# Order of units and start conditions at the opening of the second half, in a one-core attention and retention layer

## Chip, cores and metric

One core of one Trainium2 chip runs the whole program. The metric is the time of one execution in microseconds on the device. The kernel before has a median of 1897.52 us over three runs (1894.42, 1897.52 and 1897.54).

## What is computed

One layer of a streaming encoder, for 2048 prompt tokens and 64 tokens of a running stream. A combined projection of the normalised input feeds differential attention (branch A), retention (branch B), a gate path for each and two merge gates. Cut from the reference:

```
h = rmsnorm(x, norm_g) @ w_in
qa, ka, va, za, qb, kb, vb, zb, ga, gb = jnp.split(h, _split_points(), axis=-1)
...
oa = diff_attn_prompt(qa, ka, va, lam, slopes)      # block-causal, 4 heads, two softmaxes each
ob, r_p = retention_prompt(qb, kb, vb, log_g)       # chunkwise recurrence, 4 heads
...
oa = (rmsnorm(oa, subln_g) * (1.0 - lam_init)).reshape(B, T, W_A) * jax.nn.silu(za)
ob = rmsnorm(ob).reshape(B, T, W_B) * jax.nn.silu(zb)
m = ga * (oa @ w_oa) + gb * (ob @ w_ob)
return x + m @ w_out
```

## The kernel before, in words

The kernel splits every fp32 operand in a high part and a low part (`h` rounded to the matmul's type, `l` the remainder) and adds three products (high times high, high times low, low times high). So each piece of a weight matrix costs a load into a staging buffer `ws` (256 KB; there are three of them), a cast on ACT that makes `wh` (line 727), and a subtraction on POOL that makes `wl` (line 748).

**Two halves.** The prompt is projected in two halves of 1024 tokens. In the first half most columns go through a Strassen-like scheme (`strassen`, line 989). In the second half (`w_stream`, list `seqs[1]`, line 2994) there are three kinds of units:

- a *wide* unit (`natural`): 512 columns of `w_in`, eight pieces of 128x512, and eight tiles of 128 tokens. A tile takes 24 matmuls of 512 columns (line 1137), three with each piece, so all eight pieces are needed within the first tile. The three wide units are the attention's v, k and q.
- a *plain* unit (`transposed`): 256 columns, four pieces of 128x2x256, and 24 matmuls for each group of 512 or 288 tokens. The first four plain units are retention's q and k.
- the *quad* at the end: the last five column blocks in seven products (line 1564).

The pieces wait in a pool of 12 `w` and 4 `wx` buffers, two for a piece, so eight pieces in all (`next_piece`). A unit gives its pieces back during its last tile.

**Beside the projection** run, on the same engines, the attention of the first half's queries and later of the second's (`attn_head`: scores at lines 1877 and 1878, the score table added and the maximum found by DVE at 1886, exponentials on ACT at 1917, transposes at 1989, products with V at 1967 to 1969) and retention in blocks of 128 tokens (`ret_block`: three row loads, scores at 2334, key transposes at 2339, products at 2358, 2368 and 2371, output transposes at 2407).

**What sets the order.** The program is written out by coroutines (`loop`, line 216). Each yields a time or a condition. `loop` resumes the first one, by priority, whose time is not after `self.pe`, the planner's own clock for TensorE. Instructions are recorded in that order, and each engine executes its list in that order. All loads and stores go through one list as well, that of SP (`ld`, line 280, and `st`, line 285): a DMA there is issued after all those ahead of it, and waits first for what it needs. The planner's constants touched here are `CALM` (18000 of its nanoseconds) and `LAND` (2000).

**Start conditions around the change.** `h_loader` loads K and V of the heads (line 280, into `K` and `V`); after the first head it waits for `CALM`. `ret_stream` waits for twice `CALM` after the first q, k and v columns are there, and then runs the first eight retention blocks, at most two at a time; the other eight follow when the second half's retention columns are done. `ret_block` has its first matmul recorded at the time that the planner gives to the landing of its rows. A query tile of attention is 256 queries of one head; `attn_head` loops over the four tiles of a head and half.

Of the kernel before, what the change touches and what calls it, by code (L numbers as in the profile page):

```python
# [43 lines left out]
LAND = 2000.0  # L44
# [3 lines left out]
CALM = 18000.0  # L48
# [124 lines left out]
class Hybrid:  # L173
# [1654 lines left out]
    def h_loader(self, half):  # L1828
        for h in range(4):
            yield from self.head_in(half, h)  # L1830
            yield from self.load_head(half, h)
            if half == h == 0:
                yield self.pe + CALM

    def chunks(self, nk):
        n = nk // 128
# [8 lines left out]
    def attn_head(self, half, h):  # L1845
        yield lambda: len(self.heads) > 0
        hd = self.heads.pop(0)
        ks = hd["ks"]
        yield hd["tk"]
        for p in range(4 * half, 4 * half + 4):  # L1850
            yield lambda: len(self.qs) > 0
            q, tq = self.qs.pop(0)
            yield tq
            pair = {"n": 0, "rows": [None, None], "e": [None, None], "t": 0.0}
            for b in range(2):
                yield from self.qk_block(h, p, b, ks, q, pair)
            self.give("q", self.pe + LAT)
            self.spawn(self.at_pv(h, p, hd, pair, p % 4 == 3), 1, "z")
        self.give("K", self.pe + LAT, 2 * (half + 1))

# [452 lines left out]
    def ret_block(self, k, t0, r, first):  # L2313
# [9 lines left out]
        self.ld(qt, self.qbT[:, :, t0:t0 + r].rearrange("h p t -> p h t"), 1 << 18)  # L2323
        self.ld(kt, self.kbT[:, :, t0:t0 + r].rearrange("h p t -> p h t"), 1 << 18)
        t = self.ld(vb, self.vbN[t0:t0 + r, :], 1 << 18)
        yield max(t, self.t_rt)
        tx = 0
        if not first:
            nc.gpsimd.tensor_mul(qx, qt, self.rxi[:, :, :r])
# [3 lines left out]
        for h in range(4):  # L2333
            nc.tensor.matmul(s3[:, h, :], kt[:, h, :], qt[:, h, :], start=True, stop=True)
            t = self.P(512)
# [38 lines left out]
        if first:  # L2374
            nc.vector.tensor_copy(state, up)
            t = self.V(512, tu)
        else:
            for h in range(4):
# [3 lines left out]
                t = self.V(128, max(tu, to))  # L2382
# [15 lines left out]
        t = self.V(80)  # L2398
# [3 lines left out]
        t = self.V(632, t2) + SLACK  # L2402
# [3 lines left out]
        for h in range(4):  # L2406
            nc.tensor.transpose(tp[:, r * h:r * h + r], o[:, 128 * h:128 * h + 128], self.ident[:r, :r])
            t = self.P(256)
        res = qk[:, 0:4 * r]
        nc.scalar.copy(res, tp)  # L2410
        t = self.A(4 * r, t)
        self.give(bank, t)
        yield t
        for h in range(4):
            rh = res[:, r * h:r * h + r]
            d3 = self.obT[h].rearrange("p (g c) -> p g c", c=GW)
            if r == 128:
                g0, c0 = t0 // 256, t0 % 256
                t = self.st(d3[:, g0, c0:c0 + 128], rh, 1 << 16)
            else:  # L2420
                t = self.st(d3[:, :, 256:GW], rh.rearrange("p (g c) -> p g c", c=8), 1 << 17)
# [12 lines left out]

    def ret_stream(self):
        yield lambda: "kqv00" in self.done
        yield self.pe + 2 * CALM
        yield from self.ret_some(0, 8)
        yield lambda: "ret1" in self.done
        yield self.marks["ret1"] + 6000  # L2440
        yield from self.ret_sample()
        yield from self.ret_some(8, 8)
        yield self.t_state
        self.st(self.o["ret_prompt"][0, 0].rearrange("h d e -> d h e"),
                self.state.rearrange("p (h e) -> p h e", h=4), 1 << 18)
# [513 lines left out]
    def w_stream(self):  # L2959
# [3 lines left out]
        m0, m1 = (None, "kqv0"), (None, "kqv1")  # L2963
# [7 lines left out]
        wide = [(va, lambda half: self.natural(half, self.fin_va(0, 4), False, True), True),  # L2971
                (ka, lambda half: self.natural(half, self.fin_qk("k", 0, 4), False, True), True),
                (qa, lambda half: self.natural(half, self.fin_qk("q", 0, 4), False, True), True)]
        first = [wva, wk, wq, m0, m1]
        seq = []
        early = [(vb, lambda half: self.natural(half, self.fin_vb(), False, True, True), True)]
# [10 lines left out]
        for base, dst, n in ((za, self.zaT, 2), (zb, self.zbT, 2), (ga, self.gaT, 4), (gb, self.gbT, 4)):  # L2987
            for g in range(n):
# [2 lines left out]
        later = [(vb, lambda half: self.natural(half, self.fin_vb(), False, True), True)]  # L2991
        plain = [(c0, lambda half, a=a: self.transposed(*a), False) for c0, a in again[:PLAIN]]
        c0s, args = zip(*again[PLAIN:])
        seqs = [first + early + seq, [plain[0], wide[0], plain[1], wide[1], plain[2], wide[2], m0, m1, plain[3],
                                      *later, (None, "nat"), (None, "ret"), *plain[4:],
                                      (c0s, lambda half: self.quad(args), "quad")]]
        self.order = [[(c[0], c[2] if len(c) > 2 else False) for c in q if c[0] is not None] for q in seqs]
# [64 lines left out]
    def z_stream(self):  # L3062
        yield lambda: len(self.fresh) == 3
        self.n_spv = 0
        yield from self.sample_attn()
        yield lambda: self.live["z"] == 0
        yield from self.attn_zone()
        self.spawn(self.ret_stream(), 5, "z")
        for half in range(2):
            yield lambda: f"kqv0{half}" in self.done  # L3070
            self.heads, self.qs = [], []
            self.spawn(self.h_loader(half), 0, "z")
            self.spawn(self.q_loader(half), 0, "z")
            for h in range(4):
                yield from self.attn_head(half, h)
        yield lambda: self.live["z"] == 0
        self.z1.close()
        self.z3 = self.es.enter_context(self.tc.tile_pool(name="p3a", bufs=1, side="right"))
        self.z3x = ExitStack()
        self.z3w = self.z3x.enter_context(self.tc.tile_pool(name="p3w", bufs=1, side="right"))  # L3080
        self.ogs = {(g, br, kp): [] for g in range(8) for br in range(2) for kp in range(2)}
        self.oput = 0
        self.wo = [[], []]
        self.spawn(self.out_prep(), 1)
# [115 lines left out]
```

## Time and profile before

| what | us |
|---|---|
| median of three runs | 1897.52 |
| the profiled execution | 1894.89 |
| its span, first to last instruction | 1893.1 |
| TensorE (PE) busy in the span | 1869.9 |
| VectorE (DVE) busy | 1341.6 |
| ScalarE (ACT) busy | 973.9 |
| GpSimd (POOL) busy | 670.9 |

The profiled execution takes 1.8 us more than its span. A busy time is a sum over instructions; on PE the matmuls overlap, so the time from one start to the next says more than an instruction's own duration. The lists "who waited for whom" give the idle time of an engine before an instruction, and what ended it. SP has no work of its own in this table: it only issues DMAs.

### The profile page before, as it was taken

How to read it: one execution, taken by the hardware profiler on the slowest of the kernel's cores; microseconds unless marked ns; L12 is line 12 of the kernel's file. 1: busy time of each engine (PE TensorE's matmuls, PEld its weight loads, DVE VectorE, ACT ScalarE, POOL GpSimd, SP SyncE). 2: the span in 40 equal slices, each digit the busy share in tenths (PEclk: the TensorE clock that was granted, in tenths of full speed). 3: DMA queues.
4: the chain of work that ended last, by engine and by line, in shares of the span. 5: the costliest groups of instructions: out<-in, count | busy, mean ns of one | idle time of the engine just before them, and what ended most of it. 6: DMA issues, size and time to landing. Idle time of an engine off the chain costs nothing.

```text
span 1893.1 us, 33045 instructions
## 1 busy us (share of the span) xinstructions
PE 1869.9 (99%) x11090; PEld 1647.9 (87%) x11090; DVE 1341.6 (71%) x3111; ACT 973.9 (51%) x2266; POOL 670.9 (35%) x729
## 2 busy tenths in 40 slices
PE   9999999999999899999999999999999999999999
PEld 7788888888888789888888899889999999999887
DVE  6765757657584767886477686578886869977664
ACT  6434544555434566555455565556666536654221
POOL 2420366555552112121311444432122646512442
PEclk9999999999999999999999999999999999999999
DMA  7654555666857867464522854945534998976542
GB/s 254 215 176 123 160 161 180 180 196 195 248 178 200 233 194 213 126 201 123 168 69 83 230 138 133 227 130 139 143 103 138 276 256 280 269 236 206 171 156 78
DMA packets 402556, 340.09 MB, mean 180 GB/s; under 512 B 85329, under 2 KB 348625, under 8 KB 401362
## 3 DMA queue, kind: packets, MB, share of 16 engines
q1 hardware_dynamic: 402386, 337.97, 61.4%
q8 instruction: 88, 1.44, 0.3%
q14 instruction: 82, 0.67, 0.1%
HBM read 218.27 MB, written 118.75 MB: 178 GB/s over the span
## 4 chain that ended last, share of the span: by engine, by line
PE 86%; DMA 6%; DVE 4%; SPq 1%; ACT 1%; issue 1%; POOL 1%; DVEq 0%; ACTq 0%; POOLq 0%
PE mm L1137 27%; PE mm L989 8%; PE tp L989 4%; PE at L1989 3%; PE s L1877 2%; PE s L1878 2%; PE s L989 2%; PE pv L1969 2%; PE pv L1968 2%; PE pv L1967 2%; PE mm L1564 2%; PE s L2793 1%; PE s L2791 1%; PE s L2792 1%; SPq L280 1%
## 5 line engine op out<-in xcount | busy, mean ns | idle before, releaser
L748 POOL TENSOR_TENSOR wl<-ws,wh 128x512 fp32r<-128x512 f32 x108 | 146.4, 1368 | 210.4 <-ACT wh L727 196.7
L1137 PE MATMUL mm<-wh,xh 128*128 128x512 f32 x504 | 204.2, 405 | 3.0 <-ACT wh L727 3.0
L1137 PE MATMUL mm<-wl,xh 128*128 128x512 f32 x504 | 198.5, 394 | 0.8 <-POOL wl L748 0.8
L1137 PE MATMUL mm<-wh,xl 128*128 128x512 f32 x504 | 198.7, 394 | 0.0
L1137 PE MATMUL mm<-xh,wh 128*128 128x288 f32 (+2 forms) x544 | 179.3, 330 | 0.0
L1137 PE MATMUL mm<-xl,wh 128*128 128x288 f32 (+2 forms) x544 | 175.7, 323 | 0.0
L1137 PE MATMUL mm<-xh,wl 128*128 128x288 f32 (+2 forms) x544 | 175.5, 323 | 0.0
L1917 ACT ACTIVATE row<-row,a_mx 128x1024 f32<-128x1024 f32 (+7 forms) x144 | 150.0, 1044 | 11.3 <-DVE a_mx L1896 11.2
L2005 DVE TENSOR_TENSOR atl<-at,ath 128x512 fp32r<-128x512 f32 (+1 forms) x144 | 92.9, 659 | 74.0 <-ACT ath L2003 73.8
L2003 ACT CAST ath<-at 128x512 fp32r<-128x512 f32 (+1 forms) x144 | 79.2, 564 | 110.4 <-PE at L1989 104.0
L1745 POOL TENSOR_TENSOR r_y<-r_y,r_sq 128x256 f32<-128x256 f32 x32 | 29.8, 931 | 286.0 <-DVE r_sq L1742 210.2
L856 POOL TENSOR_TENSOR wl<-ws,wh 128x256 fp32r<-128x256 f32 x64 | 55.2, 862 | 196.2 <-ACT wh L847 196.0
L1886 DVE CUSTOM_DVE_ANT_0 row<-s,dfar 128x512 f32<-128x512 f32 (+2 forms) x148 | 91.5, 632 | 37.5 <-PE s L1878 36.6
L1137 PEld LDWEIGHTS mm<-wh,xl 128*128 128x128 f32 x504 | 95.0, 188 | 21.6
L1137 PEld LDWEIGHTS mm<-wh,xh 128*128 128x128 f32 x504 | 95.1, 189 | 20.7 <-ACT wh L727 3.3
L1137 PEld LDWEIGHTS mm<-wl,xh 128*128 128x128 f32 x504 | 95.4, 189 | 18.4 <-POOL wl L748 1.2
L1137 PEld LDWEIGHTS mm<-xh,wh 128*128 128x128 f32 x544 | 102.5, 188 | 7.4
L1137 PEld LDWEIGHTS mm<-xl,wh 128*128 128x128 f32 x544 | 102.5, 189 | 7.1
L1137 PEld LDWEIGHTS mm<-xh,wl 128*128 128x128 f32 x544 | 102.4, 188 | 6.7
L1939 DVE SCALAR_TENSOR_TENSOR row<-row,a_w 128x1024 f32<-128x1024 f32 (+5 forms) x88 | 98.8, 1128 | 0.0
L1877 PE MATMUL s<-K,q 128*128 128x512 f32 (+3 forms) x241 | 91.7, 381 | 0.2 <-DVE a_acc L1886 0.2
L727 ACT CAST wh<-ws 128x512 fp32r<-128x512 f32 x111 | 66.9, 617 | 41.0 <-DMA ws<-in_w_in_dram 11.2
(543 smaller groups left out, 6077.3 us busy)
## 6 DMA issues: line engine op xcount, KB each, us to landing
ws<-in_w_in_dram SPq DMA_DIRECT2D x155, 256.0 KB, 3.5
q<-qT SPq DMA_DIRECT2D x128, 128.0 KB, 3.1
K<-kT SPq DMA_DIRECT2D x48, 256.0 KB, 4.6
V<-vN SPq DMA_DIRECT2D x24, 512.0 KB, 5.5
row<-in_x_prompt_dram SPq DMA_DIRECT2D x16, 512.0 KB, 4.5
wz<-in_w_in_dram SPq DMA_DIRECT2D x32, 256.0 KB, 4.2
row<-in_cache_k_T_dram SPq DMA_DIRECT2D x32, 256.0 KB, 3.3
row<-in_cache_v_diff_dram SPq DMA_DIRECT2D x32, 256.0 KB, 3.6
```

What stands on the lines that cost most here:

```text
L727: self.nc.scalar.copy(h, st)
L748: eng.tensor_sub(l, st, h.bitcast(F32))
L856: nc.gpsimd.tensor_sub(l[:, cs], src, h[:, cs].bitcast(F32))
L989: nc.tensor.matmul(ps, w[:, c], xs[x][c], start=bool(tag) and c == 0 and i == 0, stop=c == 3 and i == 2, skip_group_check=True)
L1137: nc.tensor.matmul(ps, p, q, start=c == 0 and i == 0, stop=c == KC - 1 and i == 2)
L1877: nc.tensor.matmul(ps, q1s, kk, start=True, stop=False)
L1886: nc.vector.tensor_tensor_reduce(out=row[:, k0:k0 + n], in0=ps, in1=tab, scale=-SLOPES[h], scalar=3.0e38, op0=ALU.add, op1=ALU.min, accum_ ...
L1917: nc.scalar.activation(u, u, AF.Exp, bias=mx, scale=-1.0, accum_out=lp[:, k:k + 1])
L1939: nc.vector.scalar_tensor_tensor(out=u0, in0=u1, scalar=w[:, 0:1], in1=u0, op0=ALU.mult, op1=ALU.add)
L1989: nc.tensor.transpose(at[:, w:w + 128], src, self.ident)
L2003: nc.scalar.copy(ah[:, :w], at[:, :w])
L2005: nc.vector.tensor_sub(al[:, :w], at[:, :w], ah[:, :w].bitcast(F32))
```

## The change

Four edits. (1) The second half opens with two plain units and then two wide ones, where plain and wide units took turns; from the third plain unit on the list is as before. (2) K and V of the second head are loaded when three query tiles of attention have had their scores recorded, and not `CALM` after the first head's. (3) Retention starts when four query tiles are recorded plus one `CALM`, and not after two `CALM`. (4) In every retention block the rows count as landing `LAND` later, so its first matmul is recorded later in the list.

```diff
@@ h_loader
             if half == h == 0:
-                yield self.pe + CALM
+                yield lambda: self.ntile >= 3
@@ attn_head
             self.give("q", self.pe + LAT)
+            self.ntile += 1
@@ ret_block
-        yield max(t, self.t_rt)
+        yield max(t, self.t_rt) + LAND
@@ ret_stream
         yield lambda: "kqv00" in self.done
-        yield self.pe + 2 * CALM
+        yield lambda: self.ntile >= 4
+        yield self.pe + CALM
@@ w_stream
-        seqs = [first + early + seq, [plain[0], wide[0], plain[1], wide[1], plain[2], wide[2], m0, m1, plain[3],
+        seqs = [first + early + seq, [plain[0], plain[1], wide[0], wide[1], plain[2], wide[2], m0, m1, plain[3],
                                       *later, (None, "nat"), (None, "ret"), *plain[4:],
                                       (c0s, lambda half: self.quad(args), "quad")]]
@@ z_stream
+        self.ntile = 0
```

Each engine executes as many instructions of each kind as before; only the order and the choice of buffers differ. Line numbers in the changed kernel: retention's and attention's lines (1877, 1878, 2334) are higher by one, lines behind `ret_stream` by two, lines behind `z_stream` by three; lines up to 1830, among them 727, 748, 1137 and 1564, keep their numbers.

**SP at the opening of the second half.** `K`, `V` and `q` rows are the attention's loads, here those of the second head and the next query tiles, `ws` rows are weight pieces (128x512 of a wide unit, 128x2x256 of a plain one), `qbT<-ev` are stores of a plain unit. Before:

```order
L280 DMA K<-kT_59 64x1024
L280 DMA K<-kT_60 64x1024
L280 DMA K<-kT_59 64x1024
L280 DMA K<-kT_60 64x1024
L280 DMA V<-vN_61 128x8x128
L280 DMA V<-vN_62 128x8x128
L280 DMA q<-qT_57 64x2x256 x2
L280 DMA q<-qT_58 64x2x256 x2
L280 DMA ws<-in_w_in_dram 128x512
```

The `ws` row is the eighth and last piece of the first wide unit. At the same place now:

```order
L280 DMA ws<-in_w_in_dram 128x512
L285 DMA qbT<-ev 128x32
L285 DMA qbT<-ev 128x256
L280 DMA ws<-in_w_in_dram 128x512 x2
L280 DMA K<-kT_59 64x1024
L280 DMA K<-kT_60 64x1024
L280 DMA K<-kT_59 64x1024
L280 DMA K<-kT_60 64x1024
L280 DMA V<-vN_61 128x8x128
L280 DMA V<-vN_62 128x8x128
```

Three weight loads (pieces 4 to 6 of a wide unit that now begins one plain unit later) stand ahead of the second head's K and V.

**SP at the end of the first wide unit.** Before, the unit that follows is plain; the `128x2x256` row is the last of its four pieces, and the `128x512` rows are of the wide unit after that:

```order
L285 DMA obT<-row 128x128 x4
L280 DMA ws<-in_w_in_dram 128x2x256
L280 DMA ws<-in_w_in_dram 128x512 x2
L285 DMA vN_61<-thi 128x512
L285 DMA out_v_prompt_dram<-raw 128x512
L280 DMA row<-qbT 128x4x128
L280 DMA row<-vbN 128x512
L285 DMA vN_62<-tlo 128x512
L280 DMA ws<-in_w_in_dram 128x512 x3
```

Now the second wide unit follows at once; the five `128x512` rows are its pieces 4 to 8, and the `V` rows are the loads of a later head:

```order
L280 DMA ws<-in_w_in_dram 128x512
L285 DMA vN_62<-tlo 128x512
L280 DMA ws<-in_w_in_dram 128x512 x2
L280 DMA V<-vN_61 128x8x128
L280 DMA V<-vN_62 128x8x128
L280 DMA row<-qbT 128x4x128
L280 DMA ws<-in_w_in_dram 128x512
L285 DMA vN_61<-thi 128x512
L285 DMA out_v_prompt_dram<-raw 128x512
L280 DMA ws<-in_w_in_dram 128x512
```

A wide unit's last five pieces are now loaded while the unit ahead of it is in its last tile, and two V loads stand between the third and the fourth of them.

**SP at the last retention block.** `row<-qbT` and `row<-kbT` are its rows, `obT` and `oaT` stores of branch results, `zbT` and `gaT` stores of plain units, `xd` stores of input sums. Before:

```order
L280 DMA q<-qT_57 64x2x256 x2
L280 DMA q<-qT_58 64x2x256 x2
L285 DMA oaT<-r_o 128x256
L280 DMA row<-qbT 128x4x128
L285 DMA zbT<-ev 128x4x8
L285 DMA zbT<-ev 128x256
```

Now:

```order
L285 DMA gaT<-ev 128x2x256
L285 DMA xd<-xa 128x4x96
L280 DMA row<-qbT 128x4x128
L285 DMA xd<-xs 128x4x96
L280 DMA row<-kbT 128x4x128
L285 DMA obT<-row 128x128 x4
L285 DMA gaT<-ev 128x4x8
L285 DMA gaT<-ev 128x256
L280 DMA q<-qT_57 64x2x256 x2
```

The four query loads no longer stand ahead of the block's last row load but behind it.

## The prediction

> **What bounds the kernel now.** First the page's busy shares, then the list of what PE waited for. The columns of the list are: waiting instruction, what came last, total us, times, longest.
>
> ```profile
> span 1893.1 us, 33045 instructions
> PE 1869.9 (99%) x11090; PEld 1647.9 (87%) x11090; DVE 1341.6 (71%) x3111; ACT 973.9 (51%) x2266; POOL 670.9 (35%) x729
> ```
>
> ```profile
> PE mm L1137 <- ACT wh L727: 3.0, 1, 3.0
> PE mm L1564 <- DVE ev L1584: 2.3, 3, 1.2
> PE s L2334 <- DMA row<-qbT: 1.8, 1, 1.8
> PE s L2334 <- DMA row<-kbT: 1.8, 1, 1.8
> PE mm L1564 <- DVE u L1584: 1.6, 2, 1.0
> PE tp L1877 <- DMA q<-qT: 1.5, 1, 1.5
> ...
> PE s L1564 <- DVE ev L1584: 1.0, 1, 1.0
> ...
> PE mm L1137 <- POOL wl L748: 0.8, 1, 0.8
> PE tp L1878 <- DMA q<-qT: 0.8, 1, 0.8
> ```
>
> PE is idle for 1893.1 - 1869.9 = 23.2 us of the whole span, and the change takes no matmul away. So an order of instructions can win only what stands in this list, and the clock that an idle stretch costs. 3.0 + 0.8 us of it is one stall at the opening of the second half, 1.8 + 1.8 us are two retention blocks, 1.5 + 0.8 us are query loads, and 4.9 us belong to the quad.
>
> I then went to each place in time order. The stretches below have start and length in us, then the busy time (and number) of PE, PEld, DVE, ACT and POOL, the granted clock, the DMA share and GB/s.
>
> ```profile
> 600.00:627.00 27.00, 24.72 (x164) 22.67 (x163) 14.59 (x62) 14.15 (x39) 3.74 (x3) 1.00 1.02 259
> 627.00:634.00 7.00, 3.16 (x13) 2.20 (x12) 4.35 (x11) 2.81 (x8) 2.50 (x2) 0.87 1.11 280
> 634.00:650.00 16.00, 16.00 (x120) 15.14 (x118) 12.13 (x30) 10.97 (x29) 1.97 (x2) 0.95 0.74 225
> 650.00:700.00 50.00, 50.00 (x297) 43.84 (x297) 36.01 (x116) 28.37 (x73) 5.17 (x5) 1.00 0.70 199
> 1405.00:1460.00 55.00, 53.41 (x423) 52.17 (x422) 39.44 (x79) 37.62 (x82) 17.00 (x13) 1.00 0.43 135
> ```
>
> From 650 us on PE is covered; before that stands the costly place. Its PE rows and the SP rows ahead of them (start, length, instruction; a wait stands in brackets):
>
> ```profile
> 617.64 0.40 PE L1137 MATMUL mm<-wh,xh 128*128 128x512 f32 x1
> 617.88 0.40 PE L1137 MATMUL mm<-wl,xh 128*128 128x512 f32 x1
> 618.11 0.40 PE L1137 MATMUL mm<-wh,xl 128*128 128x512 f32 x1
> ...
> 630.81 0.50 PE L1137 MATMUL mm<-wh,xh 128*128 128x512 f32 x1 [2.99 <-ACT wh L727]
> 632.15 0.80 PE L1137 MATMUL mm<-wl,xh 128*128 128x512 f32 x1 [0.85 <-POOL wl L748]
> ```
>
> ```profile
> 616.49 2.39 SPq L280 DMA_DIRECT2D K<-kT  x4
> 618.92 1.21 SPq L280 DMA_DIRECT2D V<-vN  x2
> 620.23 4.98 SPq L280 DMA_DIRECT2D q<-qT  x4
> 625.31 0.54 SPq L280 DMA_DIRECT2D ws<-in_w_in_dram  x1
> ```
>
> ACT's cast is named, but it had waited itself: SP issued the eighth weight piece of the first wide unit only at 625.31, after 2.39 + 1.21 + 4.98 = 8.6 us of K, V and query loads, some of which waited for their buffers. The matmul that needs the piece began at 630.81, 5.5 us after that issue. So the bound here is **the order of SP's list**, not ACT or POOL. Starts of matmuls with 512 columns are 618.11 - 617.88 = 0.23 us apart at full clock.
>
> **The change part by part.** *Plain units first, second head later.* Three of the first wide unit's last loads now stand ahead of the second head's K and V, and its remaining two come with over 6 us to spare before the matmuls that need them, by counting the PE rows between at their spacing. So this stall goes: 2.99 + 0.85 = 3.84 us. With it goes the lower clock behind it: the rows give 0.87 over 7 us and 0.95 over 16 us, or 7 x 0.13 + 16 x 0.05 = 1.7 us. Together **-5.5**. What is late next is the query loads' wait of 1.5 + 0.8 us just before, whose rows ahead are the same in both orders; I leave it as it is.
>
> *Retention's rows count as landing later.* The two blocks wait here:
>
> ```profile
> 1211.72 1.13 PE L2334 MATMUL s<-row 128*128 128x128 f32 x8 [1.84 <-DMA row<-kbT]
> 1248.24 1.13 PE L2334 MATMUL s<-row 128*128 128x128 f32 x8 [1.84 <-DMA row<-qbT]
> ```
>
> In the order before, the two smallest distances between the earliest place where SP can issue a block's rows and their first use, counted in PE's work, are 7.9 and 9.9 us, and these two blocks wait. In the changed order the smallest are 9.0 and 10.3, all others 12.5 or more. By the old waits 7.9 + 1.84 = 9.7 and 9.9 + 1.84 = 11.7 were needed. But part of that need was SP's: at the second block four query loads stood ahead of the row load.
>
> ```profile
> 1239.32 3.24 SPq L280 DMA_DIRECT2D q<-qT  x4
> 1242.66 0.54 SPq L285 DMA_DIRECT2D oaT<-r_o  x1
> 1243.31 0.38 SPq L280 DMA_DIRECT2D row<-qbT  x1
> ```
>
> These 3.24 us are behind the row load now. So I take both waits as gone, **-3.7** (bounds: -3.7 and 0). The cover is projection and attention matmuls that PE has to do anyway; if it is too thin, 1.84 us stay each.
>
> *A new neighbour: wide after wide.* Before, each wide unit was followed by a plain one, which needs four pieces. Now the second wide unit follows the first at once, and its first tile needs eight pieces while the buffers hold eight and are given back only in the first unit's last tile. The trace of before has no such switch, so I build it from groups. The groups' columns are busy time, mean ns of one, and idle time before them; the DMA row ends with the median landing time.
>
> ```profile
> L748 POOL TENSOR_TENSOR wl<-ws,wh 128x512 fp32r<-128x512 f32 x108 | 146.4, 1368 | 210.4 <-ACT wh L727 196.7
> ...
> L1745 POOL TENSOR_TENSOR r_y<-r_y,r_sq 128x256 f32<-128x256 f32 x32 | 29.8, 931 | 286.0 <-DVE r_sq L1742 210.2
> ...
> L727 ACT CAST wh<-ws 128x512 fp32r<-128x512 f32 x111 | 66.9, 617 | 41.0 <-DMA ws<-in_w_in_dram 11.2
> ...
> ws<-in_w_in_dram SPq DMA_DIRECT2D x155, 256.0 KB, 3.5
> ...
> V<-vN SPq DMA_DIRECT2D x24, 512.0 KB, 5.5
> ```
>
> With time zero at the start of the last tile: the matmuls of its second piece have run by about 3.5, so the cast (0.62) and the subtraction (1.37) of the new second piece end at 5.5. That frees a staging buffer for piece 5: issue 0.5, landing 3.5, so 9.5. Its w buffers come free only at about 10.8; cast and subtraction end at 12.8, and only then piece 8 can be loaded: 12.8 + 4.0 = 16.8, cast at 17.4. POOL is then still at piece 7 and an `r_y` row of 0.93, and the eighth subtraction ends at 20.5 to 21.3. PE has, from the tile's start to the use of that piece, 104 matmul rows in the changed order: 50 of 512 columns at 0.23 (11.6), 2 of 384 at 0.18 (0.4), 20 of 256 at 0.12 (2.4), 20 of 128 at 0.11 (2.2) and 12 of retention that take two passes (2.6), about 19.2 in all. So PE waits 1.3 to 2.1; I take **+1.7**. Two more ends: nothing, if the staging turns faster; and more, if the two V loads in SP's list are slow ahead of the last pieces. The chain has one such load:
>
> ```profile
> 604.63 8.48 DMA V<-vN
> ```
>
> Then piece 8 lands at 12.8 + 8.5 = 21.3 and is ready with 0.62 + 1.37 + 0.93 at 24.2, a wait of 5.0. A wait of 2.99 brought the clock's 1.7 us above, so that end is +6.7.
>
> The clock, against the rows: a wait of 2.99 us was followed by 0.87 and 0.95; both waits of 1.84 us lie in stretches at 1.00:
>
> ```profile
> 1208.00:1214.00 6.00, 4.16 (x37) 3.96 (x36) 1.98 (x6) 1.83 (x4) 4.23 (x10) 1.00 0.71 181
> 1246.00:1250.00 4.00, 2.16 (x16) 1.75 (x15) 1.47 (x1) 0.62 (x1) 1.39 (x2) 1.00 0.97 252
> ```
>
> The Trainium skill, "TensorE: Matmul & The Clock Gate", section "What's actually happening", says that the array falls back to half its clock after an idle window of about 3.4 us, with a window that runs freely. Here an idle time of 2.99 us, shorter than that window, was enough, so the measurement decides and the threshold lies between 1.84 and 2.99 us in this trace. By the page's window the wide switch's 1.7 us would cost no clock, and a 5.0 us wait an estimated 1.7 more; the sum is the same either way.
>
> *The quad.* Attention is delayed by the later second head and so lies longer beside the quad, whose matmuls waited for DVE: 55.00 - 53.41 = 1.6 us in 1405 to 1460. By the order, the quad's matmuls ahead of the last product with V go from 234 to 276 of 840, and the common stretch from about 50 to 65 us. At 1.6 us in 55 that is **+0.5**. Below it is bounded by -1.6 (attention's extra work fills what the quad waits for), above by +3, if the rate doubles.
>
> *What else moves.* All of SP's list between 600 and 1250 us is in another order, and the trace of before has no wait from 650 to 1200 to take with it. A new one can be nothing, or as large as the one that goes, 5.5. I take **+1.0**, by the row that is nearest to a small displacement, POOL's 0.8.
>
> *The sum:* -5.5 - 3.7 + 1.7 + 0.5 + 1.0 = **-6.0**. The profiled execution took 1894.9 us (span 1893.1 and 1.8 around it), so 1888.9 for its like. The median of the runs is 1897.5, 2.6 above the profiled one; the same change there gives **1891.5**.
>
> **The rivals.**
> (a) *Retention still waits.* The rows move in the list, but their issue on SP moves too, behind stores that wait for their results, and the 1.84 us stay twice. For it: the new smallest distances, 9.0 and 10.3, are still below the needs of before, 9.7 and 11.7. Against it: the four query loads are out of the way. 1891.5 + 3.7 = 1895.2.
> (b) *The wide switch costs more.* V in front: 6.7 in place of 1.7, so 1896.5. For it: V loads do stand between the third and the fourth of the last five pieces. Against it: V's median landing is 5.5, not 8.48.
> (c) *The blocked list moves and does not go.* This is the one on the other side. In the changed order weight loads stand behind query, K or V loads or stores that wait for PE at three places of the opening: two pieces behind two queries, two stores of `qbT` and one of `oaT`; one piece behind two queries; one behind a V row. If SP stands there as it stood at 620.23 (4.98 us), each costs what the old place cost, 5.5. It decides from two places on: with two, 1897.5 - 5.5 - 3.7 + 11.0 + 1.5 = 1900.8, barely slower; with all three, 1906.3 (the third place is the wide switch, so its 1.7 isn't added; 1.5 is the quad and the rest). For it: the mechanism is the one the trace shows, and the DMA share is 1.02 and 1.11 in 600 to 634. Against it: by the PE rows each of these pieces has several us to spare, and the plain units need four pieces, not eight.
>
> **How the numbers follow.** The forecast has 0.50, with a range of its own from 1888 (no wide wait, no other) to 1895 (one more small wait and the quad's upper end). (a) has 0.12, (b) 0.12, (c) 0.26, mostly with all three. A measurement of this kernel can tell about 0.2%, 3.8 us, from no change: faster is below 1893.7, slower above 1901.3. Most of the forecast's range is faster (0.47), a rest of 0.03 with (a) and (b) is the same (0.27), and (c) is slower (0.26). The range must take in most of (c), so it goes from 1887 to 1906.5.
>
> **What would show it.** Right, if PE's list has no L1137 wait of 3 us near 630 us and a clock of 1.00 there; if L2335 (retention's line now) has no DMA wait; if the switch from the first to the second wide unit, near 720 us, shows a wait of 1 to 2 us named after ACT's cast or POOL's subtraction; and if the quad's waits for DVE sum to about 5.4. Wrong, if SP shows waits of several us at query or K loads between 570 and 660 us with a weight load behind them and PE idle after it: that is (c). Idle time of 5 us at the wide switch is (b). A time that falls without any of these places changing would mean that the sum's terms are not the ones that matter.

## The result and the profile after

The changed kernel takes a median of 1890.56 us (9 runs, 1889.51 to 1893.57), the kernel before 1896.68 us in the same series (9 runs, 1893.37 to 1897.54). The ratio is 0.9974, with a 95% interval from 0.9964 to 0.9985. The forecast was 1891.5.

The profiled execution of the changed kernel took 1890.56 us. First its busy shares, then the list of what PE waited for (columns as before: total us, times, longest):

```profile
span 1888.8 us, 33022 instructions
PE 1869.9 (99%) x11090; PEld 1647.0 (87%) x11090; DVE 1328.1 (70%) x3110; ACT 975.9 (52%) x2266; POOL 673.6 (36%) x730
```

```profile
PE at L1564 <- DVE ev L1584: 1.8, 1, 1.8
PE s L2669 <- DVE ga L2682: 1.7, 1, 1.7
PE mm L1137 <- POOL wl L748: 1.7, 2, 1.0
PE tp L1878 <- DMA q<-qT: 1.5, 1, 1.5
PE tp L1719 <- DVE u L1584: 1.1, 1, 1.1
PE s L2670 <- DVE ogl L2626: 1.1, 1, 1.1
...
PE mm L1564 <- DVE ev L1584: 0.8, 2, 0.5
PE at L2670 <- DVE ogl L2626: 0.6, 2, 0.4
```

PE's busy time is the same to the tenth, and its idle time fell from 23.2 to 1888.8 - 1869.9 = 18.9 us. The wait for ACT's cast (3.0), the two for retention's rows (1.8 each) and one for POOL (0.8) are no longer in the list. Three are new: 1.7 us for POOL's subtraction, and 1.7 and 1.1 + 0.6 us for DVE in the output stage (L2669 and L2670). The counts of two engines differ by one from before (DVE x3111 to x3110, POOL x729 to x730): one weight subtraction of the quad went from DVE to POOL, so not quite every engine executes as many instructions as before.

Not all of the 4.3 us between the two spans is the change's. PE executes the same instructions in the same order up to 616.9 us, but a matmul of line 989 that starts at 541.00 us before starts at 539.94 us here, so 1.1 us was there before the change begins.

The stretches that the prediction named (busy times of PE, PEld, DVE, ACT and POOL, then the granted clock, the DMA share and GB/s):

```profile
600.00:627.00 27.00, 25.00 (x154) 22.70 (x153) 15.13 (x62) 14.41 (x40) 5.03 (x4) 0.94 0.99 262
627.00:634.00 7.00, 7.00 (x56) 6.85 (x56) 4.67 (x12) 3.62 (x9) 1.25 (x1) 1.00 1.13 243
...
735.00:780.00 45.00, 43.34 (x265) 37.57 (x264) 35.26 (x105) 25.39 (x64) 11.34 (x10) 1.00 0.69 201
1208.00:1214.00 6.00, 6.00 (x47) 5.64 (x47) 4.16 (x13) 3.79 (x9) 1.29 (x1) 1.00 0.78 229
1246.00:1250.00 4.00, 4.00 (x29) 3.62 (x28) 3.90 (x15) 3.14 (x11) 2.06 (x6) 1.00 0.01 2
```

In 627 to 634 us PE is busy for all of 7.00 us where it had been for 3.16, and the clock is 1.00 there. Both retention places are full. What these stretches still lose lies in 735 to 780 us (1.7 us idle) and in 600 to 627 us (2.0 us idle and a clock of 0.94).

**The new wait at the switch.** The chain of waits at the place where the second wide unit follows the first (start, length, what):

```profile
735.61 4.42 DMA ws<-in_w_in_dram
740.09 0.94 POOL wl L748
741.03 4.81 DMA ws<-in_w_in_dram
...
746.56 1.26 POOL wl L748
748.16 0.73 POOL r_y L1745
748.89 1.24 POOL wl L748
```

It reads as the prediction built it: a subtraction frees a staging buffer, a load follows, the next subtraction frees the next buffer, and the eighth piece's subtraction stands behind an `r_y` row. PE's matmul with it starts at 750.17.

**The output stage.** The first product with the output weights, by the first start in these two groups (the columns are duration min, median and max in ns, then first and last start), before and after:

```profile
L2667 PE MATMUL s<-ogh,w_o_diffh x8: 283/283/288, 1538.8 to 1544.2; 128*128 128x264 f32 x8
```

```profile
L2669 PE MATMUL s<-ogh,w_o_diffh x8: 282/286/390, 1530.4 to 1536.4; 128*128 128x264 f32 x8
```

PE reaches this stage 8.4 us earlier. The end of the span comes only 1893.1 - 1888.8 = 4.3 us earlier, so 4.1 us are given back within the last 360 us. The chain of waits of the changed kernel says where nearly half of it goes:

```profile
1539.46 3.75 DMA ga<-gaT
1543.44 0.52 ACT ga L2637
1543.98 0.44 DVE ga L2682
1544.47 0.39 PE s L2669
```

The first gate's load (`ga`) is issued at 1539.46 where it had been at 1544.40, only 4.9 us earlier, because the list of SP puts it behind the last stores of the quad and the loads of the branch results. The products come 8.4 us earlier, so PE now waits for the gate's multiplication. An early start isn't the only way to that wait: start_only (below) reaches the stage at 1542.4 us, later than the kernel before, and waits 3.3 us. What goes with the wait is the distance from the first product to the issue of the gate's load. It is 5.6 us before, 9.0 in the changed kernel and 10.4 in start_only; the five kernels with 7.6 us or less (before, order_only, no_land, land_only, ret_calm2) don't wait for the gate, and the nine with 8.4 us or more do.

### The profile page after: what moved, and what is told of

It reads as the page before. It is cut to its first block, busy times and chain, and to the rows that moved or that the text cites. A ratio compares the mean times of both kernels' runs of the same rounds, so it can differ in the third digit from the quotient of the medians.

```text
span 1888.8 us, 33022 instructions
## 1 busy us (share of the span) xinstructions
PE 1869.9 (99%) x11090; PEld 1647.0 (87%) x11090; DVE 1328.1 (70%) x3110; ACT 975.9 (52%) x2266; POOL 673.6 (36%) x730
## 4 chain that ended last, share of the span: by engine, by line
PE 84%; DMA 6%; DVE 5%; issue 1%; POOL 1%; ACT 1%; SPq 1%; DVEq 0%; POOLq 0%; ACTq 0%
PE mm L1137 29%; PE mm L989 8%; PE tp L989 4%; PE at L1990 3%; PE s L1878 2%; PE s L1879 2%; PE s L989 2%; PE pv L1970 2%; PE pv L1969 2%; PE pv L1968 2%; PE mm L1564 2%; PE s L2793 1%; PE s L2795 1%; PE s L2794 1%; PE pv L2256 1%
## 5 line engine op out<-in xcount | busy, mean ns | idle before, releaser
L748 POOL TENSOR_TENSOR wl<-ws,wh 128x512 fp32r<-128x512 f32 x109 | 151.7, 1403 | 232.8 <-ACT wh L727 232.1
L1137 PE MATMUL mm<-wh,xh 128*128 128x512 f32 x504 | 203.5, 404 | 0.0
L1137 PE MATMUL mm<-wl,xh 128*128 128x512 f32 x504 | 198.1, 393 | 1.7 <-POOL wl L748 1.7
L1137 PE MATMUL mm<-wh,xl 128*128 128x512 f32 x504 | 198.3, 393 | 0.0
L1137 PE MATMUL mm<-xh,wh 128*128 128x288 f32 (+2 forms) x544 | 179.1, 329 | 0.0
L1137 PE MATMUL mm<-xl,wh 128*128 128x288 f32 (+2 forms) x544 | 176.0, 323 | 0.0
L1137 PE MATMUL mm<-xh,wl 128*128 128x288 f32 (+2 forms) x544 | 175.9, 323 | 0.0
L1137 PEld LDWEIGHTS mm<-wh,xl 128*128 128x128 f32 x504 | 94.7, 188 | 21.5
L1137 PEld LDWEIGHTS mm<-wl,xh 128*128 128x128 f32 x504 | 95.1, 189 | 19.7 <-POOL wl L748 2.5
L1137 PEld LDWEIGHTS mm<-wh,xh 128*128 128x128 f32 x504 | 94.9, 188 | 17.4 <-DVE raw L1308 0.2
L1137 PEld LDWEIGHTS mm<-xh,wl 128*128 128x128 f32 x544 | 102.6, 189 | 6.7
L1137 PEld LDWEIGHTS mm<-xh,wh 128*128 128x128 f32 x544 | 102.6, 189 | 6.5
L1137 PEld LDWEIGHTS mm<-xl,wh 128*128 128x128 f32 x544 | 102.7, 189 | 6.3
```

What stands on the lines that cost most here:

```text
L748: eng.tensor_sub(l, st, h.bitcast(F32))
L1137: nc.tensor.matmul(ps, p, q, start=c == 0 and i == 0, stop=c == KC - 1 and i == 2)
```

## The experiments

The edits are called 1 (order of units), 2 (second head), 3 (retention's start) and 4 (rows land later). The lost time below is worked out from the trace: the distance from one PE start to the next, less the median distance after an instruction of the same line and size in that kernel, summed over a stretch. It takes in waits and the lower clock alike. How sizes are grouped shifts the column 650-1150 by about 1 us in all kernels alike, so only differences between kernels are read. The first 550 us are all but the same program in every kernel and lose 8.6 to 13.7 us, so a difference of some 2 us in one profile says nothing by itself; the medians come from 6 to 12 runs. Lost times and waits come from one execution each, and some lie far from their kernel's median: land_half's took 1904.88 us, the longest of its twelve, ret_land's 1892.26, the shortest of its twelve, and no_order's 1894.44, the longest of its six.

| kernel | edits | median us | ratio to before (95% interval) | 600-650 | 650-1150 | 1150-1250 | 1250-1550 | 1550-1700 |
|---|---|---|---|---|---|---|---|---|
| before | none | 1896.7 | | 9.2 | 3.9 | 4.2 | 7.2 | 0.3 |
| order_only | 1 | 1895.3 | 0.9988 (0.9979 to 0.9997) | 7.9 | 3.8 | 3.1 | 8.8 | 0.7 |
| head_only | 2 | 1895.7 | 0.9988 (0.9978 to 0.9998) | 7.3 | 7.3 | -0.2 | 6.1 | 4.9 |
| land_only | 4 | 1903.1 | 1.0035 (1.0024 to 1.0045) | 11.6 | 7.3 | -0.2 | 13.1 | 3.0 |
| start_only | 2, 3 | 1903.5 | 1.0031 (1.0023 to 1.0040) | 5.1 | 11.5 | 8.4 | 3.6 | 5.3 |
| head_land | 2, 4 | 1895.5 | 0.9990 (0.9980 to 1.0000) | 5.6 | 9.6 | -0.1 | 8.3 | 1.5 |
| ret_land | 3, 4 | 1896.8 | 0.9999 (0.9987 to 1.0011) | 7.8 | 6.4 | -0.2 | 6.6 | 1.5 |
| no_land | 1, 2, 3 | 1902.0 | 1.0022 (1.0013 to 1.0032) | 3.8 | 12.8 | 3.7 | 8.0 | 0.7 |
| no_order | 2, 3, 4 | 1889.8 | 0.9960 (0.9948 to 0.9972) | 6.3 | 5.1 | -0.1 | 8.7 | 2.6 |
| the changed kernel | 1 to 4 | 1890.6 | 0.9974 (0.9964 to 0.9985) | 4.7 | 7.0 | 0.1 | 8.4 | 2.5 |
| land_half | 1 to 4, half of 4 | 1898.1 | 1.0012 (1.0003 to 1.0022) | 5.2 | 9.9 | 0.3 | 9.8 | 7.1 |
| land_double | 1 to 4, twice 4 | 1896.1 | 0.9996 (0.9987 to 1.0004) | 3.4 | 9.4 | -0.1 | 7.9 | 4.3 |
| ret_calm2 | 1 to 4, later start | 1902.8 | 1.0030 (1.0019 to 1.0041) | 4.9 | 13.6 | -0.1 | 11.5 | 2.9 |
| plain3_between | 1 to 4, other order | 1899.8 | 1.0016 (1.0008 to 1.0025) | 3.1 | 11.6 | -0.2 | 8.2 | 5.2 |

**Theories.** A: the gain is the sum of two kinds of stalls that go (the weight piece, and retention's rows) less the new wait at the switch. B: edit 2 alone removes the weight piece's stall, and the order of units is not needed. C: each edit shifts the work of the other streams against the projection, and the small waits that come up elsewhere are as large as those that it removes. D: the gain comes from retention's start, edit 3, which alone makes edit 4 a gain.

### order_only: edit 1 on the kernel before

```diff
-[plain[0], wide[0], plain[1], wide[1], plain[2], wide[2], m0, m1, plain[3],
+[plain[0], plain[1], wide[0], wide[1], plain[2], wide[2], m0, m1, plain[3],
```

> The kernel before with edit 1 alone (two plain units, then two wide ones). Theory A (the gain is two stalls on SP's list, the weight piece near 630 us and two retention blocks near 1211 and 1248 us, less a new wait at the switch from the first to the second wide unit): a plain unit needs only four pieces, so the stall of 3.84 us near 630 us goes although the second head is loaded early, the switch costs 1 to 2 us, retention's waits may stay: 2 to 4 us below the kernel before, ratio about 0.998 to 0.999. Rival B (the later load of the second head is what removes the stall, and the order of units only adds the switch): PE still waits 3 us or more for a weight piece within 600 to 660 us, and the time is 0 to 2 us above the kernel before.

Measured: 0.9988, about 2 us below. The longest wait of PE within 600 to 660 us:

```profile
PE s L2334 <- DMA row<-kbT: 2.8, 1, 2.8
```

The wait for the weight piece is gone without edit 2, as A said and against B. The switch from wide to wide costs nothing here: in 660 to 800 us PE has no wait that the list shows, where A had 1 to 2 us. But retention's first block waits 2.8 us for its rows at 639.7 us, in almost the same place. The old stall was exchanged for another that comes from the same crowded stretch.

### start_only: edits 2 and 3 on the kernel before

```diff
-                yield self.pe + CALM
+                yield lambda: self.ntile >= 3
...
+            self.ntile += 1
...
-        yield self.pe + 2 * CALM
+        yield lambda: self.ntile >= 4
+        yield self.pe + CALM
...
+        self.ntile = 0
```

> The kernel before with edits 2 and 3 alone (the second head is loaded at three query tiles, retention starts at four and 18 planner microseconds). In its list of SP the eighth piece of the first wide unit stands ahead of the second head's K and V. Theory A: the wide unit still opens the half as second unit and its eighth piece is still loaded late, so some 1 to 3 us of the stall stay; time 2 to 4 us below. Rival B: the stall goes entirely, there is no switch from wide to wide, and the time is 5 us or more below the kernel before, as low as the changed kernel.

Measured: 1.0031, 6 us above the kernel before, which neither theory had. The waits of PE over the whole run:

```profile
PE s L2335 <- DMA row<-qbT: 3.5, 1, 3.5
PE s L2669 <- DVE ga L2682: 3.3, 1, 3.3
PE tp L2408 <- DVE r_sq L1739: 2.7, 1, 2.7
```

No L1137 wait is left near 630 us, so at its own place edit 2 does what B says, without edit 1. What its profile has in addition are waits of retention (3.5 us for rows at 1167 us, and transposes that wait 2.7 for DVE at 751 us) and of the output's gate (3.3).

### land_only: edit 4 on the kernel before

```diff
-        yield max(t, self.t_rt)
+        yield max(t, self.t_rt) + LAND
```

> The kernel before with edit 4 alone (a retention block's rows count as landing 2 planner microseconds later). Theory A: the waits of 1.8 us at two blocks go, the stall of 3.84 us near 630 us and its low clock stay: 3 to 4 us below the kernel before, ratio 0.998. Rival B (these waits go in the changed kernel because everything around them moved, not because of edit 4): a wait of 1 us or more for a retention row stays in the list, and the time is within 1.5 us of the kernel before.

Measured: 1.0035, 6 us above. In the list of the whole run:

```profile
PE mm L1564 <- DVE ev L1584: 3.5, 2, 2.7
PE s L2667 <- DVE ev L1584: 3.2, 1, 3.2
PE s L1877 <- DVE a_acc L1886: 2.4, 3, 1.2
PE mm L1137 <- ACT wh L727: 2.3, 1, 2.3
```

No wait for rows is left (4.2 lost us in 1150 to 1250 became none), as A said of the place. The time went the other way: attention waits 2.4 us for DVE's maxima, and the quad and the first output product 6.7 us for DVE's evictions.

### no_order: the changed kernel without edit 1

```diff
-[plain[0], plain[1], wide[0], wide[1], plain[2], wide[2], m0, m1, plain[3],
+[plain[0], wide[0], plain[1], wide[1], plain[2], wide[2], m0, m1, plain[3],
```

> The changed kernel without edit 1: edits 2, 3 and 4 with plain and wide units in turns. Theory A: the switch from wide to wide (1.7 us of waits in the changed kernel) goes, but the eighth piece of the first wide unit comes late again, with 1 to 3 us of waiting near 630 us: within 2 us of the changed kernel, ratio to the kernel before about 0.997 to 0.998. Rival B (edit 1 is not needed): no wait near 630 us, none at the switch, and the time is 1.5 to 3 us below the changed kernel, ratio about 0.996.

Measured: 0.9960, 1889.8. Its profiled execution lies well above its median, so only the places are read from it; within 600 to 660 us PE's longest wait was the known one for queries,

```profile
PE tp L1878 <- DMA q<-qT: 1.7, 1, 1.7
```

and it waited for no weight piece. B is right: the order of units isn't needed for the gain. Whether it costs anything is open: the median is 0.8 us below that of the changed kernel, where B had 1.5 to 3, and the interval overlaps.

### no_land: the changed kernel without edit 4

```diff
-        yield max(t, self.t_rt) + LAND
+        yield max(t, self.t_rt)
```

> The changed kernel without edit 4: edits 1, 2 and 3. Edits 2 and 3 alone had cost about 6 us and edit 4 alone about 6 us, while 2, 3 and 4 together won about 7. Theory A (edit 4 covers retention's rows, and without it the later retention waits for rows again): PE waits 1 us or more for retention rows (L2335) at one or more blocks between 1150 and 1250 us, 3 to 8 us above the changed kernel. Rival C (the sums of small waits are a lottery of the schedule, the edits have no effects of their own): some other figure, with waits for DVE and no wait for rows.

Measured: 1.0022, 11 us above the changed kernel. PE's waits in 650 to 1300 us:

```profile
PE s L2335 <- DMA row<-kbT: 6.7, 3, 2.9
PE s L2335 <- DMA row<-qbT: 0.9, 1, 0.9
```

This is A's row wait, and more of it than in the kernel before (7.6 us at four blocks against 3.6 at two): 1.95 and 0.92 us at the blocks near 1215 and 1253 us, and 2.85 and 1.88 us at two earlier ones, near 723 and 770 us. With retention started by edit 3, edit 4 is what covers its rows.

### head_land: edits 2 and 4 on the kernel before

```diff
-                yield self.pe + CALM
+                yield lambda: self.ntile >= 3
...
+            self.ntile += 1
...
-        yield max(t, self.t_rt)
+        yield max(t, self.t_rt) + LAND
...
+        self.ntile = 0
```

> The kernel before with edits 2 and 4 (second head later, rows count as landing later; retention starts at the old time, units in the old order). Theory A (edit 2 removes the stall for the weight piece, edit 4 the waits for rows, edit 3 is not needed): as fast as edits 2, 3 and 4 together, about 7 us below the kernel before, ratio 0.996 to 0.997. Rival D (edit 3 is what makes edit 4 a gain, since it keeps retention out of the attention's way): the waits of attention for DVE near 680 and 725 us that edit 4 alone showed are there, and the time is above the kernel before by 2 us or more.

Measured: 0.9990, between the two. The weight piece's wait and the waits for rows are both gone; within 630 to 690 us the products with V wait instead:

```profile
PE pv L1968 <- ACT ath L2004: 3.1, 2, 1.9
```

So A's two terms can be had and still come to 1 or 2 us. D's waits near 680 us are there, though for ACT's cast and not for DVE's maxima, and its bound of 2 us above the kernel before was missed.

### ret_land: edits 3 and 4 on the kernel before

```diff
-        yield self.pe + 2 * CALM
+        yield lambda: self.ntile >= 4
+        yield self.pe + CALM
...
+            self.ntile += 1
...
-        yield max(t, self.t_rt)
+        yield max(t, self.t_rt) + LAND
...
+        self.ntile = 0
```

> The kernel before with edits 3 and 4 (retention starts with the query tiles, rows count as landing later; the second head is loaded at the old time, units in the old order). Theory A (the stall near 630 us is the second head's loads on SP): the wait of PE for a weight piece near 630 us is there with its low clock, 5 us, the waits for rows are gone; 2 to 4 us below the kernel before. Rival D (edit 3 makes the gain, not edit 2): 6 us or more below the kernel before and no wait near 630 us.

Measured: 0.9999. Within 600 to 660 us:

```profile
PE mm L1137 <- ACT wh L727: 1.5, 1, 1.5
...
PE mm L1137 <- POOL wl L748: 0.8, 1, 0.8
```

Without edit 2 the weight piece's wait is there (1.5 + 0.8 us, against 3.0 + 0.8), so edit 2 or edit 1 is needed for that place: A. The clock behind it stayed at 1.00 (630 to 637 us), so the place didn't cost A's 5 us, and A's 2 to 4 us below the kernel before were missed. D falls: edits 3 and 4 alone gain nothing.

### head_only: edit 2 on the kernel before

```diff
-                yield self.pe + CALM
+                yield lambda: self.ntile >= 3
...
+            self.ntile += 1
...
+        self.ntile = 0
```

> The kernel before with edit 2 alone (the second head is loaded at three query tiles). Theory A: the eighth piece of the first wide unit is loaded ahead of the second head's K and V, the wait of 3 us near 630 us goes, the waits for rows stay: 3 to 6 us below the kernel before. Rival C: other waits of the same sum come up in 700 to 900 us or at retention's last blocks, as with edits 2 and 3 together, and the time is within 2 us of the kernel before or above it.

Measured: 0.9988. No weight piece is waited for near 630 us; retention's product waits 1.4 us there for ACT, and the output's gate is waited for:

```profile
PE s L2668 <- DVE ga L2681: 3.1, 1, 3.1
...
PE at L2359 <- ACT row L2350: 1.4, 1, 1.4
```

Against the expectation the waits for rows are gone without edit 4 (4.2 lost us in 1150 to 1250 became -0.2): the shift of the attention alone had moved them. C has the better of it.

### land_half and land_double: half and twice of edit 4, in the changed kernel

```diff
-        yield max(t, self.t_rt) + LAND
+        yield max(t, self.t_rt) + LAND / 2
```

```diff
-        yield max(t, self.t_rt) + LAND
+        yield max(t, self.t_rt) + 2 * LAND
```

> The changed kernel with half of the added landing time (1 planner microsecond in place of 2; without any it had taken 1902.0, with it 1890.6). Theory A (edit 4 gives retention's rows the time that they need, so a part of it leaves a part of the waits): waits for rows (L2335) of 1 to 4 us in all stay, 1892 to 1899 us. Rival C (the time is a lottery of the order): no relation to the row waits; anything between 1889 and 1904, with the waits at other instructions.

> The changed kernel with twice the added landing time (4 planner microseconds). Theory A: waits for rows are gone already with 2, so no gain for them; the time is within 2 us of the changed kernel. Rival C: as large a change as other shifts gave, 4 us or more either way, from waits at other instructions (attention for DVE, the quad, the output's gates).

Measured: 1898.1 and 1896.1, both 5 us or more above the changed kernel. Largest waits of the first:

```profile
PE s L2669 <- DVE ga L2682: 3.0, 1, 3.0
PE s L2669 <- DVE ev L1584: 2.5, 1, 2.5
PE tp L1719 <- DVE ev L1584: 2.0, 1, 2.0
```

and of the second:

```profile
PE mm L1137 <- POOL wl L748: 3.4, 4, 1.7
PE s L2669 <- DVE ga L2682: 1.9, 1, 1.9
```

Neither list has a wait of 1 us for a retention row (land_half has one of 0.4): half of the added time covers nearly all. So the size that edit 4 has is not what the rows need. The rest is C: the wait at the switch was larger in both (2.5 us with half of the time, 3.4 with twice), and with half of it attention's end and the output stage waited 7.5 us for DVE.

### ret_calm2: a later start of retention, in the changed kernel

```diff
-        yield self.pe + CALM
+        yield self.pe + 2 * CALM
```

> The changed kernel with retention's start 18 planner microseconds later still (twice that constant after four query tiles). Theory D (what edit 3 gives edit 4 is a start of retention after the attention's opening; a later one is as good): within 2 us of the changed kernel, no wait for rows. Rival C: 4 us or more away from it, from waits elsewhere.

Measured: 1.0030, 12 us above the changed kernel, and again without row waits:

```profile
PE s L2669 <- DVE ev L1584: 3.5, 1, 3.5
PE tp L1340 <- DVE raw L1325: 3.1, 2, 1.8
PE mm L1564 <- DVE ev L1584: 2.4, 2, 1.6
PE tp L1719 <- DVE a_acc L1887: 1.9, 1, 1.9
```

All four are waits for DVE, at four unrelated places. C.

### plain3_between: another order of units, in the changed kernel

```diff
-[plain[0], plain[1], wide[0], wide[1], plain[2], wide[2], m0, m1, plain[3],
+[plain[0], plain[1], wide[0], plain[2], wide[1], plain[3], wide[2], m0, m1,
```

> The changed kernel with its units in the order plain, plain, wide, plain, wide, plain, wide: no wide unit follows a wide one. Theory A (the two waits of 1.7 us in all for POOL's subtraction near 748 us come from the switch from wide to wide): no wait of L1137 for POOL or ACT in 640 to 800 us, and 1.5 to 2.5 us below the changed kernel, about 1888.5, ratio 0.996. Rival C: the switch's waits go, but others of that sum come, and the time is 1890 us or more.

Measured: 1899.8. In 640 to 800 us the list has only a query wait of 0.6, so the waits for POOL there did come from the switch. But the edit was not what its expectation says: the next unit in the list, retention's v columns (`later`), is wide too, and with the fourth plain unit moved forward it follows the third wide unit directly. In 800 to 1050 us:

```profile
PE mm L1137 <- POOL wl L748: 2.7, 3, 1.6
PE tp L1340 <- DVE raw L1325: 1.3, 1, 1.3
```

The wait for POOL moved with the switch, to 950 to 959 us, and was larger. So these waits belong to a wide unit behind a wide one, but that order doesn't set their size: the kernels that have it wait for weights there not at all (order_only), or for 0.6 us (no_land), 0.7 (ret_calm2), 1.7 (the changed kernel), 2.5 (land_half), 2.7 (this one) and 3.4 (land_double). The total again is C's.

## Why the prediction was right, and where it was not

**The stall at 630 us** (-5.5): right in its mechanism. The wait of 3.84 us and the clock behind it are gone, no weight load is late, and four kernels without edit 1 (head_only, head_land, start_only, no_order) show that loading ahead of the second head's K and V is enough. The size came out smaller, 9.2 - 4.7 = 4.5 us of lost time, because the query wait just before it, which was to stay as it is, now carries a low clock of its own (last section). The prediction credited edits 1 and 2 together; order_only, head_only and no_order show that either is enough.

**Retention's rows** (-3.7): both waits went, 4.2 - 0.1 = 4.1 us. That edit 4 did it in this kernel is shown by no_land, where both blocks wait again (1.95 and 0.92 us), and two more. Rival (a) is out. But head_only removes the same two waits without edit 4, so the distances that the prediction counted between load and use hold for one order only.

**The switch** (+1.7): PE waited 1.7 us for POOL near 750 us, with the chain that was drawn. That the size was met to the tenth is luck: the same switch cost nothing in order_only and 3.4 us in land_double. Rival (b) is out: the two V loads did not delay the pieces. Loads took 4.4 to 4.8 us with their issue where the sum had 4.0.

**The quad** (+0.5): wrong in sign, within its bounds. Its waits for DVE were 2.3 + 1.6 + 1.0 = 4.9 us and are 1.8 + 1.1 + 0.8 = 3.7 (the 1.1 is at L1719, a matmul of the normalisation that waits for the quad's work on DVE). The common stretch did grow as predicted, from 53 to 66 us, because the quad begins 15 us earlier (1388.6 us), but it did not set the waits.

**New waits** (+1.0): this term was too small, and its place was not foreseen. The output stage takes 1888.8 - 1530.4 = 358.4 us after 1893.1 - 1538.8 = 354.3; the waits at L2669 and L2670 (1.7 + 1.1 + 0.6) are most of that 4.1. A matmul that comes too soon after its load's issue is the kind of stall that the prediction looked for only between 600 and 1250 us.

**Rival (c)**, on the other side, did not happen: SP did stand for 6.72 us at four query loads (issue from 621.28), longer than before, but no piece behind them was late.

**The sum** was -6.0; the medians differ by 6.1 us and the ratio gives 0.9974 x 1896.7 - 1896.7 = -4.9. That agreement is better than the reasoning deserved. By the two profiles the terms were -4.5 - 4.1 + 1.7 - 1.2 + 4.1 = -4.0: two gains of the predicted kind, the switch as forecast, a quad that went the other way, and an output stage that took back four times the +1.0. The terms were added as if the edits acted at their own places. By the ratios, edit 4 adds 0.35% to the kernel before and takes 0.71% from edits 2 and 3; edit 3 adds 0.43% to edit 2 and takes 0.30% from edits 2 and 4. Edit 1 makes -0.12% on the kernel before (order_only, whose interval just excludes no change), and -0.09% and +0.14% in two pairs whose intervals overlap. Three changes of one constant in the changed kernel, each of which leaves the weight piece near 630 us and all but 0.4 us of the rows covered, cost 5.5, 7.5 and 12.2 us. So the places were predicted, while the net of all other small waits is a draw, of 5 to 12 us in these three, that the views of the profile before do not hold. Why edits 2, 3 and 4 together draw so well is not settled: the attention's last product with V comes at 1455 to 1459 us in the three fastest of these kernels and at 1474 to 1485 us in five of the six slowest, which fits the waits for DVE in the quad; but no_land, the sixth, ends it at 1461, head_land and ret_land at 1461 and 1460 gain little, the kernel before ends it at 1457, and head_only, as fast as head_land, at 1477. A run that holds the attention's end and moves only retention wasn't tried.

## What to carry to other kernels

When one list sets the order for every engine, count a stall's removal as a gain at its own place, and expect the shift to cost or win about as much again elsewhere: here 5 to 12 us on 1890, as large as the gain or larger. Test each edit alone and together before crediting one, read the granted clock before crediting a few us to any, and move a constant both ways; if half and twice both lose, its value is a draw, not a fit. Look at the next stage too: its first matmuls may come sooner than its own loads allow.

## What the hardware showed

The prediction read a threshold for the clock from three waits, between 1.84 and 2.99 us. That is wrong: the length of a wait doesn't decide. In all fourteen traces, between the first and the last few us of the span, the clock is halved for 3.41 us or for twice that, and the starts of these stretches lie whole multiples of 3.41 us apart. In land_half they are 619.07, 759.02, 1455.34 and 1557.73 us, which is 41, 204 and 30 times 3.4133 us from one to the next. So the clock is set for one stretch of a fixed grid at a time, and the grid lies differently against the span's start in each trace. Here are the two waits that the threshold can't explain, split at the grid (the first number behind the length is PE's busy time, the clock is the third from the end). In the changed kernel PE waited 1.48 us up to 614.94:

```profile
612.15:615.57 3.42, 1.69 (x13) 1.32 (x11) 0.56 (x1) 1.30 (x3) 3.26 (x3) 1.00 0.66 185
615.57:618.98 3.41, 3.41 (x12) 3.12 (x13) 2.07 (x8) 0.00 (x0) 0.00 (x0) 0.50 0.77 218
618.98:622.39 3.41, 3.41 (x22) 2.98 (x22) 2.08 (x8) 2.73 (x7) 0.24 (x1) 1.00 0.96 272
```

In start_only it waited 2.73 us up to 751.64:

```profile
747.11:750.52 3.41, 1.79 (x10) 1.18 (x9) 0.55 (x3) 0.07 (x1) 1.29 (x1) 1.00 0.67 192
750.52:753.94 3.42, 2.30 (x13) 2.03 (x14) 2.39 (x7) 1.50 (x3) 1.25 (x1) 1.00 0.77 244
```

The short wait and its small neighbours fell into one stretch, which was busy for 1.69 of 3.42 us (49%), and the next stretch ran at half the clock, a loss of 3.41 / 2 = 1.7 us. The long one was split over two stretches of 53% and 67%, and the clock stayed. I split all fourteen traces this way. Of the 7684 stretches at full clock, all 22 in which PE was busy for less than 46% were followed by half the clock, 8 of the 23 between 46 and 54% were, and none of the rest. The stretches of 49 and 53% above lie in the band that can go either way; a wait of 2.73 us inside one stretch would have left it under 25%. The two waits of 1.84 us in the kernel before lie in stretches of 46 and 51%, and the 2.99 us near 630 in one of 15%. So the price of a wait of 1.5 to 3 us is nothing or 1.7 us, by where it falls in the grid and what other idle time falls beside it.

This is a part of the draw. The granted clock, in the mean of a kernel's runs, is 0.9987 in the changed kernel, 0.9977 to 0.9980 in the kernel before, and 0.9967 in ret_calm2, and 0.001 of the span is 1.9 us. So by an estimate from these means, 1 to 2 us of the change's gain and near 4 of ret_calm2's 12.2 us are the clock.

The Trainium skill, "TensorE: Matmul & The Clock Gate", section "What's actually happening", describes a free-running window of 3413 ns, and the 3.41 us here agrees with it. It names an idle window as the condition for half the clock; here a window that was half busy could be enough, so the measurement decides.
